# Retention's queries and keys two chunks a load, earlier loads of biases, second halves and gates, weight steps three behind, another order of w_out's buffers

## The chip, the cores and the metric

The kernel runs on one core of one Trainium2 chip. The metric is the time of one execution on the device, in microseconds (us). The core has a matrix engine (PE), a vector engine (DVE), a scalar engine (ACT), GpSimd (POOL) and SyncE (SP). In this kernel SP issues all DMAs, one after the other in one queue.

## The reference

One block of a hybrid model on x of 1024 tokens by 1024 channels, fp32:

```
xn = rmsnorm(x, norm1_g)
qa,ka,va, qr,kr,vr, gr, gate_a, gate_b = split(xn @ w_in)
qa = rmsnorm(qa, q_norm_g); ka = rmsnorm(ka, k_norm_g)        # 12 heads of 128
o, lse = dilated_group(qa, ka, va)                            # 3 groups x 4 slots, blocks of 128 queries
o_a = sum over groups of softmax(lse) * o
o_r = head_groupnorm(retention(qr, kr, vr)) * silu(gr)        # 4 heads, 8 chunks of 128 tokens
y = sigmoid(gate_a) * (o_a @ w_proj_a) + sigmoid(gate_b) * (o_r @ w_proj_b)
x = x + y @ w_out
x = x + square(relu(rmsnorm(x, norm2_g) @ w_up)) @ w_down
```

The three groups have dilations 1, 4 and 16. A block of 128 queries attends to its own and the previous block of 128 keys of its dilated sequence, with a bias by distance (ALiBi). Retention runs chunk by chunk with a state that decays per head.

## The kernel before

**Arithmetic.** Every fp32 product is three passes of a rounded type: an operand is split in a high and a low half, and hi·hi, hi·lo and lo·hi are summed. `split` (L344 to 350) does this: ACT copies the high half (L347), DVE subtracts it for the low half (L350). All the big matmuls are issued at L244, in `Pipe`. The large projections use seven products instead of eight (Strassen's scheme, `product` from L395); a unit is seven products named N1 to N7, and its sums run over ACT (L416, L421, L424) and DVE (L425, L430).

**Stages**, in the order of PE: the values of attention; the combined input projection ("in", 36 units); in its second half, from product 138 on, the attention core between the projection's products; retention (L897 to 1062); projection A (L1065 to 1100), of attention's output; projection B (L1101 to 1201), of retention's; w_out (L1204 to 1290); then up and down.

**Who orders what.** PE runs in the order of the program. The instructions of ACT, DVE and SP are ordered by a planner when the kernel is built, by estimates of when they will be ready, except that those marked `late` or `keep` (`tc.keep_in_program_order`) stay behind the instruction that precedes them on their engine. At run time each engine takes its queue strictly in that order, SP too: a load that stands behind a store waits until the store's data is there. A tile of a pool has a fixed number of buffers (`bufs`); a load into one waits until the readers of its earlier content are done.

**Weights.** `Weights` (L37 to 221) streams weights in a list of steps. A raw tile of 512 KB is loaded (`load`, L172 to 186, the DMA at L182) into one of three or four raw places; a step splits raw data into one of six buffers of high and low halves (0 to 5). A step needs its buffer free (`claim`), its raw tile loaded, and a clock of products that stands at least `lag` behind the load (`pump`); `pace` is how many steps may go at one tick. The units of "in", "up" and B take four steps each, named A (buffers 0, 1 in turn), B (2, 3), C (5) and D (half of 4). The lag is 2 in "in" and, from L1074 on, in both projections; it is 0 again from L1198. The eight weight tiles of w_out, four for each half of its columns, get their buffers at L387.

**Attention core.** `plan_core` (L691 to 780) puts events at numbered products; a head has nine products, starting at p0 = 138 + 9n. For head n, `prepare` (L702) loads its bias of 128 × 256 into the only bias tile, at p0 − 1. `bring` (L709) loads half c of the head's queries and keys (L713, 512 KB, two buffers) and a row of reciprocal norms broadcast to all partitions, `rb` (L715, 512 KB, one buffer), at p0 − 4 + 4c. `scale` (L719, L723) multiplies them on DVE, in place. `fetch` (L729) loads values. A block's scores are at L660, its bias is added and its minimum taken at L663 (DVE), its exponential at L665, its transpose at L671, its product with the values at L681, copied out at L684; pairs of blocks are stored at L686. `combine` mixes the three groups of a slot (loads L464, transposes L506, store L509). Heads run by slot, in the order of groups 1, 2, 0. In group 2, of dilation 16, a block has no previous block, so only 128 columns of the bias are used (`w` at L663).

**Retention.** `load_chunk` (L914 to 925) loads queries `rqT` and keys `rkT` of one chunk, 128 KB each and three buffers each (L922), and gates `sr` (L924), two chunks ahead. `decay` multiplies keys with queries (L956), masks them into `sm` (L957), splits the queries and transposes the keys (L967). At the last chunk of the last head the first three gates of projection A are loaded (L1061).

**Projection A.** 16 steps; each loads the gate tile some steps ahead (`loaded`, L888, four buffers; L1075 allows one more load at each step), multiplies its product with the gate (L1083, DVE) and stores it (L1084).

**w_out.** For each half of the columns, eight token tiles of 24 matmuls; term k takes the weight tile k // 2. At the last token tile of a half the four buffers are freed one after the other.

Of the kernel before, what the change touches and what calls it, by code (L numbers as in the profile page):

```python
# [17 lines left out]
P = 128  # L18
# [7 lines left out]
RH = 4  # L26
# [267 lines left out]
def hybrid_block(ctx: ExitStack, tc: tile.TileContext, a: dict, out: bass.AP):  # L294
# [61 lines left out]
    rc = const.tile([P, 3, RH], F, name="rc")  # L356
    gng = const.tile([P, 2, NF], F, name="gng")
    gqk = const.tile([P, 2, HEADS], F, name="gqk")
    const.tile([P, 200], F, name="rest")

    def rsqrt(dst, src, scale):
        w = src.shape[1]
# [21 lines left out]
    W.add_units("pb", [a["w_pb_q"][j] for j in range(8)])  # L384
    for nb in range(2):
        for u in range(4):
            W.add(a["w_out"][nb, u], (4, 3, 5, 2)[u] if nb else (5, 2, 0, 1)[u])  # L387
    NU, RING = FF // 256, 10
    W.add_units("up", [a["w_up"][j] for j in range(NU)])
    NC = FF // 512  # L390
# [253 lines left out]
    def attend(n, b, bias, qk, V, acc, core):  # L644

        slot, g = heads[n]
        h = g * SLOTS + slot
        nk = 2 if has_prev(g, b) else 1
        w = nk * P
        st = {}  # L650
        pair, acc = acc, acc[:, b % 2]

        def scores():
            sp = tr.tile([P, 4, P], F, name="tr")[:, :nk].rearrange("p a b -> p (a b)")
            q = qk[b // 4][:, 0, b % 4 * P:b % 4 * P + P]
            at = 0
            for c in range((b + 1 - nk) // 4, b // 4 + 1):
                n0, n1 = max(b + 1 - nk, 4 * c), min(b + 1, 4 * c + 4)
                to = slice(at, at + (n1 - n0) * P)
                nc.tensor.matmul(sp[:, to], q, qk[c][:, 1, (n0 - 4 * c) * P:(n1 - 4 * c) * P], start=True, stop=True)  # L660
                at = to.stop
            s = st["p"] = core.tile([P, 2 * P], F, name="s", bufs=3)
            nc.vector.tensor_tensor_reduce(s[:, :w], sp, bias[:, 2 * P - w:], op0=OP.add, op1=OP.min,  # L663
                                           scale=1.0, scalar=3.0e38, accum_out=acc[:, DH:DH + 1])
            nc.scalar.activation(s[:, :w], s[:, :w], AF.Exp, scale=-1.0, bias=acc[:, DH:DH + 1],  # L665
                                 accum_out=acc[:, DH + 1:DH + 2])

        def turn(bank):
            tp = bank[:, 1:]
            for j in range(nk):  # L670
                nc.tensor.transpose(tp[:, j], st["p"][:, j * P:(j + 1) * P], ident)  # L671

        def turned(bank):
            st["t"] = core.tile([P, 2, P], F, name="pT", bufs=2)
            nc.scalar.activation(st["t"][:, :nk], bank[:, 1:1 + nk], AF.Copy)

        def values(bank):
            po = bank[:, 0]
            for j in range(nk):
                k = b + 1 - nk + j  # L680
                nc.tensor.matmul(po, st["t"][:, j], V[k // 2][:, k % 2], start=(j == 0), stop=(j == nk - 1))  # L681

        def valued(bank):
            nc.scalar.activation(acc[:, :DH], bank[:, 0], AF.Copy)  # L684
            if b % 2:
                nc.sync.dma_start(tokens(acc_d[:, h, :], g, b - 1), pair)  # L686

        return scores, turn, turned, values, valued
# [4 lines left out]
    def plan_core():  # L693
# [5 lines left out]
        def late(ins):  # L699
            tc.keep_in_program_order(ins)  # L700

        def prepare(n):  # L702

            slot, g = heads[n]
            bias = core.tile([P, 2 * P], F, name="bias", bufs=1)
            late(nc.sync.dma_start(bias, a["c_bias"][g * SLOTS + slot]))
            tiles[n][0] = bias

        def bring(n, c):  # L709

            x = core.tile([P, 2, 512], F, name="qk", bufs=2)
            rb = core.tile([P, 2, 512], F, name="rb", bufs=1)
            late(nc.sync.dma_start(x, qk_d[n, :, :, 512 * c:512 * c + 512]))  # L713
            src = rs_d[n, 0, 512 * c:512 * c + 512]
            late(nc.sync.dma_start(rb, bass.AP(tensor=src.tensor, offset=src.offset, ap=[[0, P], [S, 2], [1, 512]])))  # L715
            tiles.setdefault(n, [None, [], {}, {}])[1].append(x)
            tiles[n][2][c] = x, rb
# [13 lines left out]
        def on(p, fn):  # L731
            events.setdefault(p, []).append(fn)
# [22 lines left out]

        for n in range(HEADS):
            p0 = FIRST + EACH * n
            on(p0 - 1, lambda n=n: prepare(n))
            for c in range(2):
                on(p0 - 4 + 4 * c, lambda n=n, c=c: bring(n, c))  # L760
                for f in range(2):
                    on(p0 - 1 + 3 * c + f * c, lambda n=n, c=c, f=f: scale(n, c, f))
            for b in range(NT):
                p, m = p0 + b, NT * n + b
                if b % 2 == 0:
                    on(p, lambda n=n, b=b: fetch(n, b))
                on(p, lambda n=n, b=b: begin(n, b))
                on(p, lambda m=m: pipe.at(3, lambda: turned(m)))
                on(p, lambda m=m: pipe.at(0, stages[m][0]))
# [136 lines left out]
    with ExitStack() as ph:  # L906
# [2 lines left out]
        p2 = pool(ret, "p22", 2, "right")  # L909
        p2b = pool(ph, "p22b", 2, "right")  # L910

        ready = {}

        def load_chunk(n):  # L914

            if n >= RH * NT:
                return
            h, c = divmod(n, NT)
            ts = slice(c * P, (c + 1) * P)
            qk = [p2.tile([P, 2, P], F, name=x, bufs=3) for x in ("rqT", "rkT")]  # L920
            for i in range(2):
                nc.sync.dma_start(qk[i], rqk_d[h, i, :, :, ts].rearrange("f p t -> p f t"))  # L922
            sr = p2.tile([P, 4, P], F, name="sr", bufs=4)
            nc.sync.dma_start(sr, sr_d[4 * h:4 * h + 4, :, ts].rearrange("f p t -> p f t"))  # L924
            ready[n] = (*qk, sr)

        load_chunk(0)
        load_chunk(1)
# [4 lines left out]
        def load_oa(s):  # L933
            raw = pr.tile([P, S], F, name="oraw")
            nc.sync.dma_start(raw, oa_d[s])
            split(*oaS[s], raw)

        for h in range(RH):
# [4 lines left out]
            for c in range(NT):  # L943
# [9 lines left out]
                def decay(c=c, h=h, it=it, qT=qT, kT=kT):  # L953
                    sp = ms.tile([P, 512], F, name="ms")
                    for f in range(2):
                        nc.tensor.matmul(sp[:, :P], kT[:, f], qT[:, f], start=(f == 0), stop=(f == 1))  # L956
                    sm = p2b.tile([P, P], F, name="sm")  # L957
                    nc.vector.tensor_tensor(sm, sp[:, :P], maskT[:, h, :], op=OP.mult)
                    it["s"] = p2.tile([P, P], R, name="smh", bufs=3), p2.tile([P, P], R, name="sml", bufs=3)
                    split(*it["s"], sm)  # L960
                    if c > 0:
                        it["q"] = p2.tile([P, 2, P], R, name="qh", bufs=3), p2.tile([P, 2, P], R, name="ql", bufs=3)
                        split(*it["q"], qT)
                    if c < NT - 1:
                        pt = tr.tile([P, 4, P], F, name="tr")
                        for f in range(2):
                            nc.tensor.transpose(pt[:, f, :], kT[:, f], ident)  # L967
                        kzh = p2b.tile([P, 2, P], R, name="kzh", bufs=3)
                        kzl = p2b.tile([P, 2, P], R, name="kzl", bufs=3)
                        nc.scalar.activation(kzh, pt[:, :2], AF.Copy, scale=rc[:, 2, h:h + 1])  # L970
                        nc.vector.scalar_tensor_tensor(kzl, pt[:, :2], rc[:, 2, h:h + 1], kzh.bitcast(F),
                                                       op0=OP.mult, op1=OP.subtract)
                        it["k"] = kzh, kzl
# [83 lines left out]
                    mix_next()  # L1057
                if h == RH - 1 and c >= 4:
                    load_oa(c - 4)
                if h == RH - 1 and c == NT - 1:  # L1060
                    gates = [loaded(pm2, sg_d[0, d, :, cs], "s0") for d, cs in work[:3]]  # L1061
                    raws = [(name, g, load_sum(pr, 0, name, g), -3) for name, g in (("N5", 0), ("N5", 1), ("N7", 0))]


    with ExitStack() as ph:  # L1065
        ES, e1, exts = None, ExitStack(), ExitStack()
        OPB = [{"N5": XS[0, 1], "N7": XS[1, 1]}, {}]
        waiting = [("N7", 1)] + [(name, h) for name in ("N1", "N2", "N6") for h in range(2)]
        W.lag, W.pace = 2, 1
        sigmoid(gates[0])  # L1070
        for n, (d, cs) in enumerate(work):
            if not cs.start:
                ua, = W.take(1)
                uh, ul = W[ua]  # L1074
            if len(gates) < len(work):  # L1075
                e, es = work[len(gates)]
                gates.append(loaded(pm2, sg_d[0, e, :, es], "s0"))
            pp = ms.tile([P, 512], F, name="ms")
# [123 lines left out]
    with ExitStack() as ph:  # L1202
# [55 lines left out]
        for nb in range(2):  # L1258
            us = W.take(4)
            ns = halves()[nb]  # L1260
            for n, t in enumerate([t for b, t in order if b == nb]):
# [3 lines left out]
                xt, y0 = ahead[NT * nb + n]  # L1265
                pm = mm.tile([P, 512], F, name="mm")
                terms = []
                for k in range(KT):
                    wh, wl = W[us[k // 2]]
                    o = (k % 2) * 512  # L1270
                    terms.append((*(x[:, k % 2, ts] for x in as_rows(YS[k // 2])), wh[:, o:o + 512], wl[:, o:o + 512]))
                ends = {2 * i + 1: (lambda i=i, us=us: W.free(us[i])) for i in range(4)} if n == NT - 1 else None
                pipe.step(pm, terms, ends)
                y = xt
                nc.vector.tensor_tensor(y, pm, xt, op=OP.add)
# [311 lines left out]
```

## Time and profile before

| what | value |
|---|---|
| median of three runs | 2217.45 us (2213.68, 2217.45, 2218.01) |
| profiled execution | 2214.82 us, span 2213.0 us |
| PE busy | 2168.8 us, 98% |
| DVE, ACT, POOL busy | 1387.4, 1128.4, 329.8 us |
| mean granted clock of PE | 0.998 |
| bytes by DMA | 359.09 MB, 162 GB/s over the span |
| attention core, first and last load of a half | 477.0 and 905.7 us |
| retention, first and last load of queries | 959.4 and 1235.7 us |
| first matmul of a chunk of retention | 964.22 us |
| first load of a w_out weight | 1443.79 us |

A profiled execution is one run. Its span counts from its first to its last instruction; what lies around it makes up the rest of its time. "Busy" of an engine is the sum of its instructions. In a timeline a row has the start in us, the duration, the engine, the line of the program, the operation, the tile written and the tiles read, and in brackets how long the engine was idle before it and what ended that wait. SPq rows are DMAs at the time that SP issued them, not when the data arrived. A row of a table of waits has the waiting instruction, what released it, the total in us, the number of waits and the longest.

### The profile page before, as it was taken

The page shows a single profiled execution, that of the slowest core. Times are in us where ns is not written, and L with a number is a line of the kernel's source. Part 1 is how long each engine was busy: PE and PEld are TensorE (multiplying, and loading weights), DVE is VectorE, ACT ScalarE, POOL GpSimd, SP SyncE. Part 2 cuts the span into 40 slices and gives each one's busy share as a digit, 9 for nine tenths or more (in the row PEclk, how much of TensorE's full clock was granted, in tenths as well). Part 3 has the DMA queues.
Part 4 walks back from the last instruction along what each step waited for, and adds up shares of the span by engine and source line. Part 5 has one row for each costly group of instructions (what it writes and reads, how often), then busy time and mean ns, then how long its engine had stood idle before and what let it go on. Part 6 is the DMA issues. An engine that isn't in the chain of part 4 may idle for free. (4 is left out here: it accounts for less than half of the span.)

```text
span 2213.0 us, 28838 instructions
## 1 busy us (share of the span) xinstructions
PE 2168.8 (98%) x9928; PEld 1783.6 (81%) x9928; DVE 1387.4 (63%) x2374; ACT 1128.4 (51%) x2145; POOL 329.8 (15%) x340
## 2 busy tenths in 40 slices
PE   8999999999999999999999999999899999999999
PEld 6888888788888877878888877878788888778787
DVE  5624555655556665658767767783855556787874
ACT  4425665534655544535555645542555455755542
POOL 1000000000000000002123110000000000677873
PEclk9999999999999999999999999999999999999999
DMA  6322333343657676664364478774245556654532
GB/s 206 132 87 82 109 100 91 101 135 115 202 176 229 202 211 193 196 189 142 113 189 126 137 253 283 264 235 148 82 139 157 157 155 193 226 174 157 178 121 105
DMA packets 294614, 359.09 MB, mean 162 GB/s; under 512 B 35058, under 2 KB 202418, under 8 KB 294211
## 3 DMA queue, kind: packets, MB, share of 16 engines
q1 hardware_dynamic: 294466, 357.25, 51.7%
q8 instruction: 78, 1.28, 0.2%
q14 instruction: 70, 0.57, 0.1%
HBM read 240.59 MB, written 116.59 MB: 161 GB/s over the span
## 5 line engine op out<-in xcount | busy, mean ns | idle before, releaser
L350 DVE TENSOR_TENSOR wl<-raw,wh 128x1024 fp32r<-128x1024 f32 (+1 forms) x308 | 343.9, 1119 | 387.6 <-ACT wh L347 386.2
L347 ACT ACTIVATE wh<-raw 128x1024 fp32r<-128x1024 f32 (+1 forms) x308 | 295.8, 963 | 291.0 <-PE ms L244 102.6
L244 PE MATMUL mm<-xh,wh 128*128 128x512 f32 x960 | 388.8, 405 | 0.4 <-DVE u L425 0.4
L244 PE MATMUL mm<-xh,wl 128*128 128x512 f32 x960 | 376.0, 392 | 1.1 <-DVE wl L350 1.1
L244 PE MATMUL mm<-xl,wh 128*128 128x512 f32 x960 | 375.3, 391 | 0.3 <-DVE xl L350 0.3
L244 PE MATMUL ms<-xh,wh 128*128 128x512 f32 x784 | 317.2, 405 | 6.9 <-ACT u L424 3.7
L244 PE MATMUL ms<-xh,wl 128*128 128x512 f32 x784 | 306.4, 391 | 0.0
L244 PE MATMUL ms<-xl,wh 128*128 128x512 f32 x784 | 305.9, 390 | 0.0
L244 PEld LDWEIGHTS mm<-xh,wl 128*128 128x128 f32 x960 | 180.8, 188 | 40.9 <-DVE wl L350 2.0
L244 PEld LDWEIGHTS mm<-xh,wh 128*128 128x128 f32 x960 | 181.3, 189 | 35.6 <-DVE u L425 0.8
L244 PEld LDWEIGHTS mm<-xl,wh 128*128 128x128 f32 x960 | 181.4, 189 | 35.1 <-DVE xl L350 0.7
L989 POOL TENSOR_TENSOR st<-st,half 128x1 f32<-128x1 f32 x32 | 26.3, 823 | 1093.2 <-DVE st L988 1093.1
L244 PE MATMUL mm<-wh,xh 128*128 128x512 f32 x458 | 186.1, 406 | 0.5 <-DVE Y L1418 0.5
L244 PE MATMUL mm<-wl,xh 128*128 128x512 f32 x458 | 178.6, 390 | 1.6 <-DVE wl L350 1.6
L244 PE MATMUL mm<-wh,xl 128*128 128x512 f32 x458 | 179.4, 392 | 0.0
L244 PEld LDWEIGHTS ms<-xh,wh 128*128 128x128 f32 x784 | 147.5, 188 | 38.8 <-ACT u L424 6.7
L244 PEld LDWEIGHTS ms<-xh,wl 128*128 128x128 f32 x784 | 147.3, 188 | 31.8
L244 PEld LDWEIGHTS ms<-xl,wh 128*128 128x128 f32 x784 | 147.7, 188 | 27.6
L244 PEld LDWEIGHTS mm<-wh,xl 128*128 128x128 f32 x458 | 85.9, 188 | 19.1
L244 PEld LDWEIGHTS mm<-wl,xh 128*128 128x128 f32 x458 | 86.5, 189 | 17.7 <-DVE wl L350 2.1
L244 PEld LDWEIGHTS mm<-wh,xh 128*128 128x128 f32 x458 | 86.2, 188 | 16.7 <-DVE Y L1418 1.3
L1418 DVE TENSOR_TENSOR Y<-Y,ms 128x512 f32<-128x512 f32 x88 | 59.7, 682 | 55.9 <-PE ms L244 55.8
(304 smaller groups left out, 3983.7 us busy)
## 6 DMA issues: line engine op xcount, KB each, us to landing
raw<-in_w_up SPq DMA_DIRECT2D x32, 512.0 KB
h_d<-s SPq DMA_DIRECT2D x64, 256.0 KB
raw<-in_w_down SPq DMA_DIRECT2D x32, 512.0 KB
raw<-in_w_aqk_q SPq DMA_DIRECT2D x24, 512.0 KB
qk_d<-sg SPq DMA_DIRECT2D x48, 256.0 KB
qk<-qk_d SPq DMA_DIRECT2D x24, 512.0 KB
rb<-rs_d SPq DMA_DIRECT2D x24, 512.0 KB
s<-sg_d SPq DMA_DIRECT2D x40, 256.0 KB
```

The source lines that it names most:

```text
L244: self.nc.tensor.matmul(ps, x, y, start=start, stop=stop, skip_group_check=not first)
L347: hi = nc.scalar.activation(dst_h, src, AF.Copy)
L350: nc.vector.tensor_tensor(dst_l, src, dst_h.bitcast(F), op=OP.subtract)
L989: nc.gpsimd.tensor_tensor(st[:, 9:10], st[:, 8:9], half[:, 0:1], op=OP.pow)
L1418: nc.vector.tensor_tensor(Y[r][:, ns], Y[r][:, ns], ps, op=op)
```

## The change

Six edits, with nothing taken from or added to the arithmetic:

1. Retention loads queries and keys for two chunks at once, at even chunks, into two buffers of 256 columns instead of three of 128; `sm` has one buffer; an unused constant of 800 bytes a partition (`rest`) goes.
2. The bias of a head is loaded at p0 − 4 instead of p0 − 1, except for every third head (n a multiple of 3); for heads of group 2 only its last 128 columns are loaded, into a tile of their own.
3. The second half of a head's queries, keys and `rb` is requested at p0 − 1 instead of p0.
4. Four gates of projection A are loaded at chunks 3 to 6 of the last head instead of three at chunk 7 and one at the first step.
5. The lag of the weight steps in both projections is 3 instead of 2.
6. The first four weight tiles of w_out go to buffers 0, 1, 5, 2 instead of 5, 2, 0, 1; the last token tile of that half takes its terms 4 to 7 ahead of 0 to 3, and frees 5 and 2 first, as before.

```
-    const.tile([P, 200], F, name="rest")
...
-            W.add(a["w_out"][nb, u], (4, 3, 5, 2)[u] if nb else (5, 2, 0, 1)[u])
+            W.add(a["w_out"][nb, u], (4, 3, 5, 2)[u] if nb else (0, 1, 5, 2)[u])
...
-            nc.vector.tensor_tensor_reduce(s[:, :w], sp, bias[:, 2 * P - w:], op0=OP.add, op1=OP.min,
+            nc.vector.tensor_tensor_reduce(s[:, :w], sp, bias[:, -w:], op0=OP.add, op1=OP.min,
...
-            bias = core.tile([P, 2 * P], F, name="bias", bufs=1)
-            late(nc.sync.dma_start(bias, a["c_bias"][g * SLOTS + slot]))
-            tiles[n][0] = bias
+            lo = P if g == 2 else 0
+            bias = core.tile([P, 2 * P - lo], F, name=f"bias{lo}", bufs=1)
+            late(nc.sync.dma_start(bias, a["c_bias"][g * SLOTS + slot][:, lo:]))
+            tiles.setdefault(n, [None, [], {}, {}])[0] = bias
...
-            on(p0 - 1, lambda n=n: prepare(n))
+            on(p0 - (4 if n % 3 else 1), lambda n=n: prepare(n))
             for c in range(2):
-                on(p0 - 4 + 4 * c, lambda n=n, c=c: bring(n, c))
+                on(p0 - 4 + 3 * c, lambda n=n, c=c: bring(n, c))
...
-            qk = [p2.tile([P, 2, P], F, name=x, bufs=3) for x in ("rqT", "rkT")]
-            for i in range(2):
-                nc.sync.dma_start(qk[i], rqk_d[h, i, :, :, ts].rearrange("f p t -> p f t"))
+            if c % 2 == 0:
+                both = [p2.tile([P, 2, 2 * P], F, name=x) for x in ("rqT", "rkT")]
+                for i in range(2):
+                    nc.sync.dma_start(both[i], rqk_d[h, i, :, :, c * P:(c + 2) * P].rearrange("f p t -> p f t"))
+                for m in range(2):
+                    ready[n + m] = [x[:, :, m * P:(m + 1) * P] for x in both]
             sr = p2.tile([P, 4, P], F, name="sr", bufs=4)
             nc.sync.dma_start(sr, sr_d[4 * h:4 * h + 4, :, ts].rearrange("f p t -> p f t"))
-            ready[n] = (*qk, sr)
+            ready[n].append(sr)
...
-                    sm = p2b.tile([P, P], F, name="sm")
+                    sm = p2b.tile([P, P], F, name="sm", bufs=1)
...
+                if h == RH - 1 and 3 <= c < NT - 1:
+                    d, cs = work[c - 3]
+                    gates.append(loaded(pm2, sg_d[0, d, :, cs], "s0"))
                 if h == RH - 1 and c == NT - 1:
-                    gates = [loaded(pm2, sg_d[0, d, :, cs], "s0") for d, cs in work[:3]]
...
-        W.lag, W.pace = 2, 1
+        W.lag, W.pace = 3, 1
...
-            if len(gates) < len(work):
+            if len(gates) < min(n + 4, len(work)):
...
-                for k in range(KT):
+                turned = nb == 0 and n == NT - 1
+                for k in (*range(4, KT), *range(4)) if turned else range(KT):
...
-                ends = {2 * i + 1: (lambda i=i, us=us: W.free(us[i])) for i in range(4)} if n == NT - 1 else None
+                ends = {2 * i + 1: (lambda u=us[i ^ 2 if turned else i]: W.free(u)) for i in range(4)} if n == NT - 1 else None
```

More of the change, by code (lines that the diff above doesn't have):

```diff
@@ L910, in hybrid_block @@
         p2b = pool(ph, "p22b", 2, "right")
-        ready = {}
+        ready, gates = {}, []
         def load_chunk(n):
```

## The prediction

> **What bounds the kernel now.** First the head of the page.
>
> ```profile
> span 2213.0 us, 28838 instructions
> PE 2168.8 (98%) x9928; PEld 1783.6 (81%) x9928; DVE 1387.4 (63%) x2374; ACT 1128.4 (51%) x2145; POOL 329.8 (15%) x340
> ```
>
> PE is idle for 2213.0 − 2168.8 = 44.2 us in all. The change takes no matmul away, so it can only give back idle PE time, or slow clock that follows it. Second, the table of what PE waited for (total, times, longest):
>
> ```profile
> PE ms L244 <- ACT u L424: 3.7, 6, 1.0
> PE mm L244 <- DVE wl L350: 2.7, 3, 1.6
> PE ms L244 <- DVE s L1083: 2.6, 2, 1.7
> PE tr L506 <- DVE acc L663: 2.5, 1, 2.5
> PE ms L956 <- DMA rkT<-rqk_d: 2.2, 1, 2.2
> PE tr L660 <- DVE acc L663: 2.0, 2, 1.3
> ```
>
> These six lines are the places that the edits can reach; together 15.7 us. Everything else is the start, up, down and the tail. Third, the stretches around each of them by timeline, quoted below (start, duration, what ran, and in brackets the idle time before it with what ended it). I make the sum against the profiled execution, which took 2214.82 us with a span of 2213.0; the three runs have their median at 2217.45, 2.63 higher. About 0.2%, 4.4 us, is what a measurement of this kernel can tell from no change.
>
> **Part 1: attention core, second halves and biases.** DVE scales queries and keys (L723) with a broadcast row `rb`, and the table of DVE's waits shows that it is often late:
>
> ```profile
> DVE qk L723 <- DMA rb<-rs_d: 21.1, 13, 3.7
> DVE s L663 <- DMA bias<-in_c_bias: 5.7, 2, 5.0
> ```
>
> PE idles for it in few places, since scores are taken well ahead of the matmuls behind them. The dear one is head 8, second half:
>
> ```profile
> 799.40 1.41 DVE L723 SCALAR_TENSOR_TENSOR qk<-qk,gqk,rb 128x512 f32<-128x512 f32 x2
> 799.30 0.35 SPq L706 DMA_DIRECT2D bias<-in_c_bias  x1
> 804.57 0.38 SPq L686 DMA_DIRECT2D acc_d<-acc  x1
> 805.04 0.53 SPq L713 DMA_DIRECT2D qk<-qk_d  x1
> 805.66 0.55 SPq L715 DMA_DIRECT2D rb<-rs_d  x1
> 813.24 0.75 DVE L723 SCALAR_TENSOR_TENSOR qk<-qk,gqk,rb 128x512 f32<-128x512 f32 x1 [3.68 <-DMA rb<-rs_d]
> 814.38 0.69 PE L506 MATMUL tr<-ident,oa 128*128 128x128 f32 x2 [2.55 <-DVE acc L663]
> 814.72 0.78 PE L244 MATMUL ms<-xh,wh 128*128 128x512 f32 x1
> 817.43 0.42 PE L244 MATMUL mm<-xh,wh 128*128 128x512 f32 x1
> 817.92 0.39 PE L244 MATMUL mm<-xh,wl 128*128 128x512 f32 x1
> 814.38:817.40 3.02, 3.02 (x8) 2.47 (x9) 1.51 (x4) 2.46 (x7) 0.00 (x0) 0.50 0.93 337
> ```
>
> The single `rb` buffer is free when the two scalings of the first half end, 799.40 + 1.41 = 800.81. SP then stands before the store L686 until 804.57, and the load of the second half is queued behind it. From its issue to the scaling pass 813.24 − 805.66 = 7.58 us. The change puts the bring one step earlier, ahead of that store: issue at about 801.4, arrival at about 801.4 + 7.58 = 809.0. DVE began to wait at 813.24 − 3.68 = 809.56 and PE at 814.38 − 2.55 = 811.83, so both waits go: **−2.55**. Behind the wait the clock was granted at 0.50 (the last row, from a table of windows: five engines' busy time, then granted clock, DMA share and GB/s). Seven matmuls start in 817.43 − 814.72 = 2.71 us; the next two, at full clock again, in 817.92 − 817.43 = 0.49, or 0.245 each, at which seven take 1.7: **−1.0**.
>
> [...]
>
> Costs of this part. The bring is now ahead of the store it used to follow, so the store, and whatever SP holds behind it, goes two issues later: 0.53 + 0.55 = 1.08 us of SP, beside work. The bias (for heads 1, 2, 4, 5 and so on) goes three steps earlier, just ahead of the first half's bring, and delays it by one issue and its bytes, 0.35 us at least. One first half is tight already:
>
> ```profile
> 868.75 0.75 DVE L723 SCALAR_TENSOR_TENSOR qk<-qk,gqk,rb 128x512 f32<-128x512 f32 x1 [3.29 <-DMA rb<-rs_d]
> 870.36 0.70 PE L660 MATMUL tr<-qk 128*128 128x256 f32 x2 [0.72 <-DVE acc L663]
> 729.70 0.71 PE L681 MATMUL tr<-V,pT 128*128 128x128 f32 x4 [0.68 <-ACT acc L684]
> 847.40 0.70 PE L660 MATMUL tr<-qk 128*128 128x256 f32 x2 [1.30 <-DVE acc L663]
> ```
>
> The 0.72 belongs to head 10 and should grow: bounds 0.35 (the issue alone) and 1.05 (with the bias's 128 KB at the 190 GB/s of a row below, 0.7); I take the middle, **+0.7**. The row at 729.70 is ACT held by a raw weight tile; weight loads now stand behind 1 MB of queries and rows more often. Bounds for that: 0 (its cover is the ~2.7 us of matmuls of one product) and 0.68 for each of the four second halves that move past one (heads 0, 2, 5 and 7 in SP's timeline), 2.7; I take 0, since only one such row exists among 24 brings, and keep the end. The bias itself gives nothing: the 1.30 at 847.40 is head 9, whose bias isn't moved (9 is a multiple of 3). The 128-column bias tile saves bytes only.
>
> **Part 2: retention's queries and keys by two chunks.**
>
> ```profile
> 959.81 0.47 SPq L922 DMA_DIRECT2D rkT<-rqk_d  x1
> 963.99 0.76 SPq L922 DMA_DIRECT2D rkT<-rqk_d  x1
> 964.22 0.61 PE L956 MATMUL ms<-rqT,rkT 128*128 128x128 f32 x4
> 969.32 0.68 PE L956 MATMUL ms<-rqT,rkT 128*128 128x128 f32 x4 [2.19 <-DMA rkT<-rqk_d]
> 950.00:1000.00 50.00, 47.81 (x232) 39.61 (x231) 27.95 (x69) 20.71 (x43) 2.42 (x3) 1.00 0.64 190
> ```
>
> Chunk 0's keys were requested at 959.81 and used without an idle row at 964.22; chunk 1's were requested at 963.99 and cost 2.19. Now chunk 1 arrives with chunk 0: **−2.19**. The first pair is twice as large: 2 × 128 KB more at the 190 GB/s of the last row is 1.4 us at most, and chunk 0's slack inside 964.22 − 959.81 = 4.4 us isn't shown. Bounds of that loss are 0 and 1.4; I take 0. Later pairs are asked for two chunks, some 20 us, ahead; that covers their size. 32 of SP's 64 issues of this kind go, each about 0.4 us beside other work: 0 on the path. One `sm` buffer instead of two (L957) makes DVE wait for the two splits of the chunk before, done a chunk earlier: 0.
>
> **Part 3: gates.**
>
> ```profile
> 1138.95 2.07 SPq L888 DMA_DIRECT2D s<-sg_d  x4
> 1297.95 0.33 SPq L888 DMA_DIRECT2D s<-sg_d  x1
> ```
>
> SP issued four gate loads together at 1138.95, 130 us ahead of their use, although the code has them at the last chunk and behind it. Asking sooner moves nothing: **0**. The 2.6 us of PE before L1083 come from later gates (the one at 1297.95), whose buffers turn over as before. Bounds 0 and −2.6.
>
> **Part 4: lag 3 in both projections.** The lag is counted when the program is written: a weight step isn't put into it until so many steps behind its load. In projection B ACT reaches a step too early and stands:
>
> ```profile
> 1425.31 1.07 ACT L347 ACTIVATE wh<-raw 128x1024 fp32r<-128x1024 f32 x1 [2.11 <-DMA raw<-in_w_pb_q]
> 1427.94 0.50 PE L244 MATMUL ms<-xh,wh 128*128 128x512 f32 x1 [1.05 <-ACT u L424]
> 1390.00:1440.00 50.00, 48.95 (x215) 39.91 (x214) 40.56 (x60) 27.43 (x46) 0.00 (x0) 1.00 0.87 296
> ```
>
> One product is about 2.7 us, more than the 2.11 that ACT stood. With the step a product later ACT has its copy L424 done first, and the 1.05 should go: **−1.05**. Bounds: −3.7 if all waits for u L424 go, and as a loss one late split (1.63, part 5) in each of eight units, +13.0. I take the row that fits.
>
> **Part 5: order of w_out's buffers.**
>
> ```profile
> 1443.79 3.33 SPq L182 DMA_DIRECT2D raw<-in_w_out  x2
> 1473.97 5.75 SPq L182 DMA_DIRECT2D raw<-in_w_out  x2
> 1483.01 1.06 ACT L347 ACTIVATE wh<-raw 128x1024 fp32r<-128x1024 f32 x1 [2.21 <-DMA raw<-in_w_out]
> 1484.60 1.22 DVE L350 TENSOR_TENSOR wl<-raw,wh 128x1024 fp32r<-128x1024 f32 x1
> 1485.87 0.50 PE L244 MATMUL mm<-wl,xh 128*128 128x512 f32 x1 [1.63 <-DVE wl L350]
> ```
>
> The first two raw tiles are in by about 1450, but their splits go to buffers 5 and 2, which the last unit of B holds to its end; so raw places turn over late, the last loads leave at 1473.97, and PE waits 1.63. Buffers 0 and 1 (the A pieces) are free earlier; two splits then run inside B and two loads leave sooner: **−1.63**. The last of the first eight steps takes rows 4 to 7 first, so buffers 5 and 2 are freed in the old order and the second half's weights keep their times: 0. Bounds: −1.63, and +2.21 if a split then stands before its own raw tile.
>
> **Sum.** −2.55 − 1.0 + 0.7 − 2.19 + 0 − 1.05 − 1.63 = −7.7: 2214.82 − 7.7 = 2207.1 for a profiled execution like this one, and 2207.1 + 2.63 = 2209.7 against the median.
>
> **Rivals.** [...] (b) *All gate and projection waits go as well.* The remaining 3.7 − 1.05 + 2.6 = 5.2 are added: −12.9, 2204.5. For it: fewer issues on SP before the gates; against it: part 3. (c) *Absorbed.* Waits move on: DVE's next wait, for a product or a raw tile, ends as late, and only retention's 2.19 with part of the rest remains: −2.8, 2214.7. For it: 21.1 us of `rb` waits that showed on PE in very few places, and DMA at 0.93 of its time in the window behind head 8, so what comes sooner is carried slower. (d) *Slower: weight splits late in projection B.* With lag 3 the A piece of a unit waits one product more, and D, B and C follow one a step. If a piece then falls to the step that needs it, PE stands for a copy and a subtraction; price 1.63, the nearest row of such a wait. DVE is busy 40.56 of 50 there, so little room is left to catch up. At one late piece in each of eight units +13.0; with the other parts, −7.7 + 1.05 = −6.7, that is +6.3, 2223.8. With four late pieces (6.5) the gain is gone, with seven (11.4) the kernel is 4.7 us slower. Against it: DVE's idle share and four raw places, which hold two units. (e) *The change doesn't do what it says*: that is already so for the gates, and is in the sum.
>
> **Chances.** Forecast 0.40, (a) 0.10, (b) 0.10, (c) 0.25, (d) 0.15. Faster by over 0.2% are the forecast, (a) and (b): 0.60. Within: 0.25. Slower: 0.15. The range reaches from (b) with the further 0.7 of a tight head 10 that could stay as it is, and some of the runs' own spread below their median, 2202, up to no change with the losses of part 1 and part 2 at their ends left half open (1.4 and some 0.7), 2219; what it leaves out is (d) and a little of (b).
>
> **What would show it.** In the changed kernel: no wait over 1 us for `rb` in a second half, and full clock at 810 to 820 us; no row of PE behind rkT at chunk 1; gate loads at about the same place and the two waits for L1083 still there; ACT no longer behind a raw tile of pb for over 2 us; the first two splits of w_out before 1475. Wrong it would be made by new PE rows "wl L350" in projection B, by PE waiting at chunk 0 of retention, or by new ACT waits for raw tiles between 550 and 930 that PE shows too.

## The result: 1% slower, and where the time went

The changed kernel takes 2238.21 us (median of four runs, 2235.0 to 2238.96) against 2216.84 for the kernel before on the same chip: a ratio of 1.0098, 95% interval 1.0084 to 1.0112, or some 22 us more where 7.7 less were forecast. The profiled execution took 2237.82 us. Head of its page:

```profile
span 2236.0 us, 28756 instructions
## 1 busy us (share of the span) xinstructions
PE 2191.4 (98%) x9928; PEld 1784.3 (80%) x9928; DVE 1387.9 (62%) x2374; ACT 1132.0 (51%) x2145; POOL 328.1 (15%) x340
```

PE is idle for 2236.0 − 2191.4 = 44.6 us, 0.4 more than before. But it is **busy 22.6 us longer with the same 9928 instructions**. So most of the loss isn't a wait, and no table of waits can show it. Here is that table for PE in the changed kernel, for what did move:

```profile
PE ms L959 <- DMA rkT<-rqk_d: 5.4, 1, 5.4
...
PE ms L244 <- ACT u L423: 2.8, 5, 0.7
PE ms L244 <- DVE s L1088: 2.6, 1, 2.6
...
PE tr L659 <- DVE acc L662: 1.4, 3, 0.8
PE tr L659 <- DVE qk L723: 1.2, 1, 1.2
...
PE ms L244 <- DVE wl L350: 1.0, 1, 1.0
```

Head 8's wait (tr L506) is gone, retention's has grown from 2.2 to 5.4 us, a wait of 1.2 for scaled queries or keys (qk L723) is new, and the others moved by some 2 us at most.

The slower matmuls show in a table of windows in which PE is busy all the time. The columns are PE, its weight loads, DVE, ACT and POOL with their counts in brackets, then granted clock, DMA share and GB/s. First the kernel before:

```profile
40.00:140.00 100.00, 100.00 (x454) 82.75 (x453) 44.06 (x63) 31.80 (x50) 0.55 (x1) 1.00 0.28 101
200.00:300.00 100.00, 100.00 (x440) 82.39 (x439) 51.98 (x68) 61.37 (x92) 0.00 (x0) 1.00 0.35 104
300.00:400.00 100.00, 100.00 (x440) 82.31 (x440) 52.05 (x69) 64.09 (x93) 0.00 (x0) 1.00 0.36 100
1650.00:1750.00 100.00, 100.00 (x443) 82.81 (x442) 56.56 (x75) 51.11 (x80) 0.00 (x0) 1.00 0.54 157
```

Then the changed one:

```profile
40.00:140.00 100.00, 100.00 (x454) 82.85 (x453) 43.92 (x63) 31.71 (x48) 0.55 (x1) 1.00 0.27 101
200.00:300.00 100.00, 100.00 (x433) 80.96 (x432) 50.77 (x68) 61.88 (x93) 0.00 (x0) 1.00 0.36 105
300.00:400.00 100.00, 100.00 (x433) 80.99 (x432) 51.37 (x68) 60.68 (x88) 0.00 (x0) 1.00 0.34 98
1650.00:1750.00 100.00, 100.00 (x435) 81.24 (x434) 56.64 (x75) 49.18 (x77) 0.00 (x0) 1.00 0.51 148
```

In the first stage (40 to 140 us) both run 454 matmuls. From 200 to 400 us, long before any edited line runs, the changed kernel does 433 in 100 us instead of 440, at full clock (1.00) and with no more DMA. In the up projection it is 435 instead of 443. That is 1.6 to 1.8% in these windows; over the whole kernel PE is busy 1.0% longer.

A timeline of PE in the up projection of the changed kernel shows that it goes by product. These are the first matmuls of three products of twelve matmuls each, one behind the other without a pause:

```profile
1656.68 0.39 PE L244 MATMUL mm<-xh,wh 128*128 128x512 f32 x1
...
1659.40 0.40 PE L244 MATMUL ms<-xh,wh 128*128 128x512 f32 x1
...
1662.20 0.40 PE L244 MATMUL mm<-xh,wh 128*128 128x512 f32 x1
```

The first product takes 1659.40 − 1656.68 = 2.72 us, as all did before; the second takes 1662.20 − 1659.40 = 2.80. They have the same shape and differ in where their operands lie. The unused constant of 800 bytes, which the change drops, lay ahead of the weight buffers and of the operands kept on the left side, so all of these moved down by 800 bytes; tiles allocated from the right side stayed. 800 is twelve times 64 and 32 more:

| built program | first weight buffer begins at | first operand, left side | an operand, right side | past a multiple of 64 |
|---|---|---|---|---|
| before | 17120 | 66272 | 212960 | 32, 32, 32 |
| changed | 16320 | 65472 | 212960 | 0, 0, 32 |

A matmul of L244 has two operands: one of 128 columns, which its row names last (here called the weights of the matmul), and one of 512 columns, which its row names first (here the moving operand). **Theory (placement):** a matmul is slower when these two lie differently within 64 bytes. The first stage multiplies left operands with left weights, alike in both kernels; the product at 1656.68 reads a left operand, the one at 1659.40 a right one. **Rival:** the reordered loads and splits slow the kernel through contention.

### The profile page after: what moved, and what is told of

It reads as the page before. It is cut to its first block, busy times and chain, and to the rows that moved or that the text cites. A ratio compares the mean times of both kernels' runs of the same rounds, so it can differ in the third digit from the quotient of the medians.

```text
span 2236.0 us, 28756 instructions
## 1 busy us (share of the span) xinstructions
PE 2191.4 (98%) x9928; PEld 1784.3 (80%) x9928; DVE 1387.9 (62%) x2374; ACT 1132.0 (51%) x2145; POOL 328.1 (15%) x340
## 5 line engine op out<-in xcount | busy, mean ns | idle before, releaser
L244 PE MATMUL mm<-xh,wh 128*128 128x512 f32 x960 | 392.1, 408 | 2.5 <-ACT ms L415 2.1
L244 PE MATMUL mm<-xh,wl 128*128 128x512 f32 x960 | 377.6, 393 | 0.3 <-DVE wl L350 0.3
L244 PE MATMUL mm<-xl,wh 128*128 128x512 f32 x960 | 376.4, 392 | 0.2 <-DVE xl L350 0.2
L244 PE MATMUL ms<-xh,wh 128*128 128x512 f32 x784 | 320.3, 409 | 6.1 <-ACT u L423 2.8
L244 PE MATMUL ms<-xh,wl 128*128 128x512 f32 x784 | 309.4, 395 | 1.0 <-DVE wl L350 1.0
L244 PE MATMUL ms<-xl,wh 128*128 128x512 f32 x784 | 308.5, 394 | 0.0
L244 PEld LDWEIGHTS mm<-xh,wl 128*128 128x128 f32 x960 | 180.5, 188 | 43.4 <-DVE wl L350 0.7
L244 PEld LDWEIGHTS mm<-xh,wh 128*128 128x128 f32 x960 | 181.0, 189 | 40.1 <-ACT ms L415 3.0
L244 PEld LDWEIGHTS mm<-xl,wh 128*128 128x128 f32 x960 | 181.2, 189 | 37.3 <-DVE xl L350 0.6
L244 PE MATMUL mm<-wh,xh 128*128 128x512 f32 x458 | 187.3, 409 | 0.5 <-DVE Y L1424 0.5
L244 PE MATMUL mm<-wh,xl 128*128 128x512 f32 x458 | 181.0, 395 | 0.9 <-DVE xl L350 0.9
L244 PE MATMUL mm<-wl,xh 128*128 128x512 f32 x458 | 180.6, 394 | 0.0
L244 PEld LDWEIGHTS ms<-xh,wh 128*128 128x128 f32 x784 | 147.4, 188 | 39.9 <-ACT u L423 5.3
L244 PEld LDWEIGHTS ms<-xh,wl 128*128 128x128 f32 x784 | 147.0, 188 | 37.0 <-DVE wl L350 1.4
L244 PEld LDWEIGHTS ms<-xl,wh 128*128 128x128 f32 x784 | 147.4, 188 | 30.3
L244 PEld LDWEIGHTS mm<-wh,xl 128*128 128x128 f32 x458 | 86.6, 189 | 20.9 <-DVE xl L350 1.4
L244 PEld LDWEIGHTS mm<-wh,xh 128*128 128x128 f32 x458 | 86.9, 190 | 18.2 <-DVE Y L1424 1.3
L244 PEld LDWEIGHTS mm<-wl,xh 128*128 128x128 f32 x458 | 87.0, 190 | 16.4
```

The lines of the kernel that those rows point to most:

```text
L244: self.nc.tensor.matmul(ps, x, y, start=start, stop=stop, skip_group_check=not first)
```

## The experiments

Ratios are against the kernel before on the same chip, with 95% intervals. Differences in us are worked out from the ratio (0.001 is 2.2 us), so the medians can differ by a little more or less.

**e1, only the constant taken out of the kernel before.**

```
-    const.tile([P, 200], F, name="rest")
```

> The kernel before, with only the unused constant of 800 bytes a partition left out, so that all tiles placed behind it lie 800 bytes lower. Theory (placement): the fp32 matmuls keep their full pace only where the moving operand and the weights lie alike within 64 bytes; before, all lie 32 bytes past a multiple of 64, without the constant the weights and some operands lie on a multiple and others do not. Expect 2216.8 + 21 = about 2238 us, and about 433 instead of 440 matmuls in each of the windows 200 to 400 us. Rival (the reordered loads of the other edits slow the kernel): no change, 2213 to 2219 us.

Measured: 2227.06 us, ratio 1.0051 (1.0036 to 1.0067), 11 us more. Its windows:

```profile
40.00:140.00 100.00, 100.00 (x455) 82.84 (x454) 43.54 (x61) 31.23 (x48) 0.42 (x1) 1.00 0.28 101
200.00:300.00 100.00, 100.00 (x433) 81.00 (x432) 50.75 (x68) 61.16 (x91) 0.00 (x0) 1.00 0.36 103
```

The slow pace is there with none of the other edits: 433. But the loss is only half of the 21 us expected, outside both forecasts. In the profiled execution (2231.91, the longest of its four) PE was busy for 2190.1 us, 21.3 more than before, as expected, and idle for 40.0 instead of 44.2: where PE is slower, it waits less for the others (in m1 below, 36.7 us against 44.3 in e4). How its other three runs (2226.5 to 2227.1) give back some 5 us more isn't shown: they have no profile.

**e2 and e3, the changed kernel with 32 and with 64 unused bytes in that place.**

```
+    const.tile([P, 8], F, name="rest")      # e2; [P, 16] in e3
```

> The changed kernel with an unused constant of 32 bytes a partition put back in the same place, so that the weights lie 32 bytes past a multiple of 64 again. Theory (placement): the 21 us go, 440 matmuls in each of the windows 200 to 400 us; what remains is the sum of the other edits, 2210 to 2218 us. Rival (the other edits slow the kernel): 2238 us as with the change.

> The changed kernel with an unused constant of 64 bytes a partition in the same place: everything moves by 64 bytes and lies within 64 bytes as in the changed kernel. Theory (place within 64 bytes): as slow as the changed kernel, 2236 to 2240 us. Rival (a boundary that the tiles of the changed kernel cross, since some begin 64 bytes ahead of a multiple of 8192): gone with the shift, 2210 to 2218 us.

Measured: e2 2218.97 us, 1.0022 (1.0013 to 1.0031); e3 2233.59, 1.008 (1.0067 to 1.0094). Windows of e2, then one of e3:

```profile
200.00:300.00 100.00, 100.00 (x441) 82.37 (x440) 51.28 (x68) 62.27 (x93) 0.00 (x0) 1.00 0.36 105
...
1650.00:1750.00 100.00, 100.00 (x443) 82.81 (x442) 56.45 (x73) 51.36 (x79) 0.00 (x0) 1.00 0.52 153
```

```profile
200.00:300.00 100.00, 100.00 (x435) 81.18 (x434) 50.83 (x68) 62.13 (x93) 0.00 (x0) 1.00 0.37 105
```

32 bytes bring the full pace back (441, 443) and take 17 of the 22 us; 64 bytes leave it slow (435). So it is the place within 64 bytes, not a boundary further out. Both times lie just outside what was expected: e2 is 1 us above its range, and e3 2.4 us below, some 4 us faster than the changed kernel; why, isn't shown. The five that remain in e2 (4.9 us) are the other edits.

**e4, the kernel before with 32 bytes instead of 800.**

```
-    const.tile([P, 200], F, name="rest")
+    const.tile([P, 8], F, name="rest")
```

> The kernel before with its unused constant cut from 800 to 32 bytes a partition: the tiles move by 768 bytes, a multiple of 64. Theory (place within 64 bytes): no change, 2213 to 2219 us. Rival (the 800 bytes set some other place, within 1024 or more): slower, up to 2238 us.

Measured: 2214.64, 0.9996 (0.9987 to 1.0005). Neither the 800 bytes nor the room they take matter, only their remainder within 64. This is the base of the runs that follow.

**m1, 32 bytes between weights and left operands.**

```
+    pool(ctx, "gap", 1).tile([P, 8], F, name="gap")
     big = pool(ctx, "big", 3)
```

> The base with 32 unused bytes a partition between the weight buffers and the operands: the weights stay 32 bytes past a multiple of 64, the operands of the left side of the memory lie on a multiple, those of the right side stay 32 past. Theory (a matmul is slower where its two operands lie differently within 64 bytes): now the matmuls of the left operands are the mixed ones, the values stage among them, which no shift has touched so far: 233 instead of 227 ns a matmul there, 8 ns less than 40 matmuls of 1000 lost in the first 100 us, 2225 to 2245 us in all. Rival (operands or weights on a multiple of 64 are slow by themselves): the values stage and the total differently, with the left operands slow only as far as the weights are, none here: 2213 to 2219.

(The expectation's "8 ns less than 40 matmuls" is badly put; 227 to 233 ns in that stage is what was expected.) Measured: 2236.85, 1.0098 (1.0084 to 1.0112).

```profile
40.00:140.00 100.00, 100.00 (x443) 80.83 (x442) 44.32 (x64) 32.22 (x50) 0.55 (x1) 1.00 0.28 100
200.00:300.00 100.00, 100.00 (x434) 80.99 (x432) 51.77 (x68) 61.78 (x93) 0.00 (x0) 1.00 0.36 101
```

This tells the two forms of the theory apart. The first stage, at 454 or 455 in every kernel so far, falls to 443. In this stage the roles are turned, as a row of m1 shows: the weight buffer `wh` is the moving operand, and `xh` the weights of the matmul.

```profile
60.11 0.40 PE L244 MATMUL ms<-wh,xh 128*128 128x512 f32 x1
```

So m1 shifts the 128-column operands there and leaves the moving ones 32 past a multiple, as in e4. From 200 us on it is the other way round: the moving operands of the left side lie on a multiple, their weights 32 past, and the count is 434, though other products are slow now than in the changed kernel. So neither side is slow by lying on a multiple of 64: alike is fast (32 with 32 before, 440 matmuls from 200 us on; 0 with 0 in the first stage of the changed kernel, 454), and unlike is slow either way round (0.233 us from start to start in the changed kernel and in m1, against 0.228 before; see the last section).

The size fits as well. By the addresses in the built programs, all 8736 matmuls of L244 read alike operands before, and 2976 of them unlike ones in the changed kernel. At the 6 ns each that the last section gives, that is an estimate of 18 us; PE is busy 20.2 us longer in the changed kernel than in e2 (2191.4 − 2171.2). In m1 4752 are unlike: 29 us by the same estimate, against 23.2 more busy time than in e4 (2196.0 − 2172.8).

**p1, only the attention core's edits.** Their diff stands in the section on the change (the lines of `bias`, `prepare` and `bring`).

> The kernel before with an unused constant of 32 bytes in place of 800 (which alone changed nothing) and only the edits of the attention core: second halves a step earlier, biases three steps earlier, 128-column biases. Theory (as predicted for this part): PE's wait of 2.55 us for head 8 and the half clock behind it go, head 10 loses some 0.7: 2.5 to 4 us less, 2211 to 2213. Rival (weight loads held up behind the earlier loads eat the gain): 2214 to 2216.

Measured: 2211.83, 0.9987 (0.9979 to 0.9996), 2.8 less. SP of p1, the load for head 8, and a window of PE there:

```profile
799.66 0.53 SPq L714 DMA_DIRECT2D qk<-qk_d  x1
801.78 0.36 SPq L716 DMA_DIRECT2D rb<-rs_d  x1
805.27 0.36 SPq L686 DMA_DIRECT2D acc_d<-acc  x1
```

```profile
800.00:820.00 20.00, 20.00 (x102) 16.79 (x100) 14.64 (x39) 10.98 (x30) 0.00 (x0) 1.00 0.68 211
```

The `rb` row leaves at 801.78, ahead of the store at 805.27; PE is busy throughout, at full clock. But p1 has a new wait at an earlier head. ACT, DVE and PE there:

```profile
562.37 1.06 ACT L347 ACTIVATE wh<-raw 128x1024 fp32r<-128x1024 f32 x1 [3.19 <-DMA raw<-in_w_gate_q]
...
568.00 0.74 DVE L724 SCALAR_TENSOR_TENSOR qk<-qk,gqk,rb 128x512 f32<-128x512 f32 x1
...
568.79 0.49 PE L660 MATMUL tr<-qk 128*128 128x128 f32 x2 [1.41 <-DVE qk L724]
```

The raw weight tile is requested at the same time as in e4 (555.35 against 555.32), but now behind the head's queries and row instead of ahead of them. ACT stands 3.19 us for it, where e4 starts the same copy at 559.13 without a wait; the splits and the scaling behind it come later, and PE stands 1.41 us. The changed kernel has this wait too (1.2, qk L723).

**p2, only retention's pairs** (the lines of `load_chunk` and `sm`).

> The same base with only retention's loads of two chunks and the single sm buffer. Theory (from the changed kernel's trace: the first pair is issued behind four other DMAs and is twice as long): PE waits 3 to 5 us at chunk 0, against 2.19 at chunk 1 before, with a stretch of half clock behind it: 2 to 4 us more, 2217 to 2219. Rival (as predicted): 2.2 less, 2213.

Measured: 2218.67, 1.0018 (1.001 to 1.0027), 4.1 more. SP and then PE of p2:

```profile
960.52 0.32 SPq L860 DMA_DIRECT2D rqk_d<-sg  x1
961.30 0.33 SPq L182 DMA_DIRECT2D raw<-in_w_rv  x1
961.90 0.32 SPq L509 DMA_DIRECT2D oa_d<-oaT  x1
962.86 0.32 SPq L860 DMA_DIRECT2D rqk_d<-u  x1
963.27 0.41 SPq L923 DMA_DIRECT2D rqT<-rqk_d  x1
963.73 0.93 SPq L923 DMA_DIRECT2D rkT<-rqk_d  x1
```

```profile
969.29 1.20 PE L959 MATMUL ms<-rqT,rkT 128*128 128x128 f32 x4 [5.14 <-DMA rkT<-rqk_d]
```

```profile
969.29:973.00 3.71, 3.71 (x12) 3.25 (x13) 1.82 (x5) 1.40 (x4) 0.00 (x0) 0.54 1.14 320
```

The planner now sets the first load behind four other DMAs that it used to precede: 963.27 instead of 959.39. From the issue of the keys to PE pass 969.29 − 963.73 = 5.56 us. In the kernel before, it was 964.22 − 959.81 = 4.41 with no wait, so the larger load takes at least 1.1 us more, and the later request makes up the rest. PE stands 5.14 us at chunk 0 and then runs at a granted 0.54. Why the planner moved the load isn't shown.

**p3, only lag 3; p4, only w_out's order; p5, only the gates** (their lines as in the change).

> The same base with only the lag of 3 in both projections. Theory (from the trace: new waits for splits and copies in projection B): 2 to 4 us more, 2217 to 2219. Rival (as predicted): the wait of 1.05 at 1427.94 goes, 1 less, 2214.

> The same base with only the new order of w_out's buffers and the turned last step. Theory (as predicted): the wait of 1.63 us for wl at 1485.87 goes, 2213.5. Rival (the splits come to stand in projection B ahead of what its units need, as the waits for xl and wl at about 1470 and 1494 in the changed kernel suggest): no gain or 1 more, 2215 to 2216.

> The kernel before with an unused constant of 32 bytes in place of 800 and only the gates of projection A requested at chunks 3 to 6. Theory (as predicted: they were asked for long before in the order that SP has): no change, 2213 to 2216 us. Rival (SP's order around projection A moves): 1 to 3 us either way.

Measured: p3 2216.18, 1.0006 (0.9997 to 1.0015), between its two forecasts and not to be told from no change; p4 2216.42, 1.001 (1.0002 to 1.0019), 2.2 more (0.4 to 4.2), on the side of its rival; p5 2214.53, 0.9997 (0.9988 to 1.0006), none. PE's waits in p3:

```profile
PE ms L244 <- ACT u L424: 4.9, 6, 1.5
...
PE ms L244 <- DVE s L1083: 2.8, 1, 2.8
```

The waits for u L424 are six as before, with 4.9 us instead of 3.7. In p4, DVE and then PE at the end of projection B:

```profile
1458.99 1.21 DVE L350 TENSOR_TENSOR wl<-raw,wh 128x1024 fp32r<-128x1024 f32 x1
1460.13 0.68 DVE L350 TENSOR_TENSOR xl<-s,xh 128x512 fp32r<-128x512 f32 x1
1460.73 2.44 DVE L350 TENSOR_TENSOR wl<-raw,wh 128x1024 fp32r<-128x1024 f32 x2
```

```profile
1462.00 0.50 PE L244 MATMUL ms<-xh,wl 128*128 128x512 f32 x1 [0.80 <-DVE wl L350]
...
1487.48 0.50 PE L244 MATMUL mm<-wh,xl 128*128 128x512 f32 x1 [0.94 <-DVE xl L350]
```

The wait of 1.63 is gone, as forecast, but two others have come: DVE has a w_out split among those that B still needs, so B's last unit waits 0.80, and w_out's first step waits 0.94 for the last split of its own operand. Together 1.74, no gain. What makes 2.2 us more of that, these two don't show.

**u1, the changed kernel with 32 bytes and without the pairs** (`load_chunk` and `sm` as before).

> The changed kernel with the constant of 32 bytes and with retention's loads of one chunk as before. Theory (the parts add up: 4.8 more than before for all, 4.1 of it from the pairs): 0 to 2 us above the kernel before, about 2215. Rival (the parts don't add up): as with the pairs, 2219, or as before less the core's gain, 2212.

Measured: 2213.8, 0.9997 (0.9988 to 1.0005). Within the intervals, of about 2 us either way each, the parts add up: −2.8 + 1.3 + 2.2 − 0.7 = 0.0, measured −0.7; and with the pairs' 4.1, 4.1 against 4.9 in e2.

**b1, the core's edits, and queries and keys of a chunk in one load.**

```
-            qk = [p2.tile([P, 2, P], F, name=x, bufs=3) for x in ("rqT", "rkT")]
-            for i in range(2):
-                nc.sync.dma_start(qk[i], rqk_d[h, i, :, :, ts].rearrange("f p t -> p f t"))
+            x = p2.tile([P, 4, P], F, name="rqk", bufs=3)
+            nc.sync.dma_start(x, rqk_d[h, :, :, :, ts].rearrange("i f p t -> p (i f) t"))
+            qk = [x[:, 0:2], x[:, 2:4]]
+            ready[n] = qk
...
-            ready[n] = (*qk, sr)
+            for m in (0, 1) if n == 1 else (n,) if n else ():
+                hm, cm = divmod(m, NT)
+                sr = p2.tile([P, 4, P], F, name="sr", bufs=4)
+                nc.sync.dma_start(sr, sr_d[4 * hm:4 * hm + 4, :, cm * P:(cm + 1) * P].rearrange("f p t -> p f t"))
+                ready[m].append(sr)
```

> The base with the edits of the attention core, and retention's queries and keys of one chunk in one load, those of chunks 0 and 1 ahead of the gates of chunk 0. In the order of SP both loads now stand ahead of the stores behind which chunk 1 stood. Theory (chunk 1 was late because its load stood behind four other DMAs): the wait of 2.2 to 2.4 us at chunk 1 goes, 2211.8 - 2.3 = 2209 to 2210 us. Rival (the bytes at that place set the time, in whatever order): chunk 0 waits instead, 2211 to 2213.

Measured: 2208.51, 0.9966 (0.9954 to 0.9978), **7.5 us below the kernel before** (4.9 to 10.2; the medians differ by 6.2) and the fastest version found. SP and PE of b1:

```profile
957.44 0.92 SPq L922 DMA_DIRECT2D rqk<-rqk_d  x2
958.79 0.33 SPq L861 DMA_DIRECT2D rqk_d<-sg  x1
```

```profile
962.27 0.61 PE L960 MATMUL ms<-rqk 128*128 128x128 f32 x4
...
965.02 0.61 PE L960 MATMUL ms<-rqk 128*128 128x128 f32 x4
```

Both chunks leave SP together, ahead of the store, and no idle time stands before either of PE's rows. This trace is of the slowest of b1's six runs (2216.31), so it shows that the wait is gone, not where the time comes from. Beyond the core's 2.8 the gain is 4.7 us, where 2.3 was expected; the surplus isn't explained. The run joins two loads, sets them ahead and lets the gates of chunk 0 wait, and no run tells these three apart.

## Why the prediction was wrong, step by step

**The step that failed isn't in the sum at all.** The prediction began with "The change takes no matmul away, so it can only give back idle PE time, or slow clock that follows it", and so took the duration of a matmul as fixed. The dropped constant got no term: its 800 bytes, and the shift of all that lies behind them, don't appear in the prediction. e1, e2 and m1 show that shift to set the pace of PE. It cost 17 us by e2 (21.7 − 4.9), and 11 by e1.

**Core, −2.85 forecast (−2.55 − 1.0 + 0.7): the main step right, the total partly by luck.** p1 has −2.8 (−4.7 to −0.9). Head 8 went as told: `rb` ahead of the store, no idle PE, full clock at 800 to 820 us. But the weight loads behind the earlier brings were taken at 0 ("only one such row exists among 24 brings"), and one of them now costs 1.41; the prediction had named it as a sign of being wrong, new ACT waits for raw tiles that PE shows too. Against it, head 10 went from 0.72 to 0.90 instead of by 0.7, and head 9's 1.30, which was to stay, isn't in p1 (in e4, without the edits, it is 0.50).

**Pairs, −2.19 forecast: +4.1.** The failed step is "Bounds of that loss are 0 and 1.4; I take 0". It priced the larger transfer and left the time of issue where it was, though SP's order is the planner's to make. The request came 3.9 us later (963.27 against 959.39 in the two traces), the transfer itself took at least 1.1 more, near the upper bound, and chunk 0 waits 5.14. b1 shows that the aim was right: with both chunks requested together, ahead of the store, the wait is gone.

**w_out, −1.63 forecast: +2.2.** The wait named did go. That "two splits then run inside B" was priced at nothing, with DVE busy 40.56 of 50 us there; two new waits of 0.80 and 0.94 took its place. The bound of +2.21 held the result, for another reason.

**Lag, −1.05 forecast: +1.3 (−0.7 to 3.3).** The term rested on one wait of 1.05 at 1427.94. In e4, the same schedule once more, that place shows 0.19, and in p3, with the lag of 3, it shows 0.68; so one row of one execution was too little, and the lag doesn't take the wait away.

**Gates, 0 forecast: right** (p5). **Rival (d), slower by late splits,** was given the right sign and the wrong place: it is seen in p4 in a small way, but not as the main cause.

## What to carry to other kernels

Removing an unused tile is a change (11 us in e1, with nothing else edited): compare the placement of operands, and the count of matmuls in windows where PE has no idle time, before explaining a difference by waits. Where PE's busy time grows at an equal count and full clock (here by 22.6 us at 9928), look for the cause in the matmuls themselves. A load made larger must be looked up in the issuing queue's new order, since its place there can cost more than its bytes (in p2 a request 3.9 us later, against at least 1.1 us for the size).

## What the runs showed of the hardware

Matmuls of 128x512 here start every 2.72 / 12 = 0.227 us when their two operands lie alike within 64 bytes, and every 2.80 / 12 = 0.233 us when they don't (the products at 1656.68 and 1659.40 of the changed kernel). Over all matmuls of L244 that are followed by another without a pause, the mean distance of the starts is 0.233 us both for the some 2490 of the changed kernel with the moving operand at 32 and the weights at 0, and for the some 2320 of m1 the other way round; in the kernel before, where all lie alike, it is 0.228. In that row of products, the one right behind an unlike one is slowed too, although alike (2.76 us for the one at 1662.20). Why the pace depends on the placement, and why the product behind is slowed, isn't shown; only multiples of 32 were tried.

Half clock followed a short wait in some executions and not in others. In the kernel before it was 0.50 after 2.55 us at head 8, second half. At the same place the granted clock in the 3 us behind the wait was, in e4 after 2.31 us,

```profile
814.26:817.30 3.04, 3.04 (x16) 2.61 (x17) 1.53 (x4) 2.56 (x8) 0.00 (x0) 1.00 0.90 326
```

and in p2 after 1.98 us:

```profile
815.65:818.60 2.95, 2.95 (x8) 2.46 (x9) 1.45 (x4) 2.46 (x7) 0.00 (x0) 0.50 0.96 345
```

So a wait of about 2 us was followed by half clock in one execution and not in the other, at the same place of the core's code. The forecast's 1.0 for it was a chance, not a fixed price.
